# Gates' sums beside the down products, sample loads on ScalarE's queue, earlier prompt loads

## Chip, cores and metric

The kernel runs on one core of one Trainium2 chip. The metric is the time of one execution on the device in microseconds (us). The median of three runs before the change is 2212.91 us.

## The reference

One layer of a hybrid decoder for 1024 prompt tokens and 32 sample tokens (8 sequences of 4), which have 2048 past positions each in pages of 128:

```python
x = x + 0.5 * SwiGLU_1(RMSNorm(x))                 # 1024 -> 2816 -> 1024
q, k, v, fl, bg, cg, u = split(RMSNorm(x) @ w_in)   # 24 tiles of 128 columns, and 8 gate logits
logf = log_sigmoid(fl + b_f)                        # per head
# attention: logit[t, s] = q_t . k_s / 8 + sum of logf over s < j <= t
# sample tokens: keys, values and logf of the past come from the pages of page_table;
# suffix = cumsum(logf_past, reverse) - logf_past
y = bg * conv3(cg * u)
x = x + concat(RMSNorm(attn), RMSNorm(y)) @ w_out
x = x + 0.5 * SwiGLU_2(RMSNorm(x))                  # then the final RMSNorm
```

Outputs are the result for prompt and sample tokens, and the new k, v, logf and conv states. The past gates' sums (`suffix`) depend on the inputs alone, on nothing that the layer computes.

## The kernel before

Every product is made of three: each fp32 operand is split into a high and a low part, and `Step.mm3` (L103 to L105) multiplies high by high, high by low and low by high. A weight is loaded by `Step.load` (L78, three buffers `wraw`), ACT makes its high part `wh` (L86), DVE its low part `wl` (L88). Activations are split the same way (L192 on ACT, L193 on DVE). Tokens stand in four chunks of 264 columns.

The program is one stream; a scheduler puts each engine's instructions in order, except PE's order from the mixing stage on, which is written out by hand. Each engine, and each engine's DMA queue, works through its own list in order. SP issues DMAs only; POOL issues its DMAs and the indirect ones (gathers).

1. **Up** (`K.up`): the first feed-forward products; the result goes in pieces of 132 KB to `h1_d` in DRAM, stored by POOL (L326, L331).
2. **Past gates** (L549 to L582): a pool `gp` on the left side, which takes the space of the up operands, so its tiles wait for them. SP loads the page table (`pt`, `ptl`) and `cin`, DVE makes indices, SP spreads them into `idl`. POOL gathers 32 pages of `lf` (L465), four to a buffer R (two buffers); DVE runs a prefix sum over 512 columns (L577), SP stores it to `bs_d` (L582).
3. **Down** (`K.down`): h comes back from `h1_d` through SP (L384), is split, and multiplied by `w2a` in four sections (`DOWN1`): chunk 0 whole; chunks 1 and 2 with f 0 to 12, then with f 12 to 22; chunk 3. Each product is added to x by DVE (L407). `done1` stores x (L597, POOL) and makes the normed operands XH and XL.
4. **Mix** (L612 on): `forget()`, then the 24 tiles of `w_in` as q, k, v and conv projections (`win`, 3 chunks of 352 columns each, PSUM tiles `pg`, three buffers). Between their steps the sample tokens' attention runs over key and value pages: every second page is loaded by SP with a page number from a register (L802, L803), the others by POOL's gathers (L465), six buffers `kvraw`. This is called the sample stretch here.
5. **Prompt attention**: rounds of logits, softmax, turn and weigh; `load_qk` and vt come by POOL, `conv_norm` of chunks 0 and 1 runs at round 9 (`CONV_AT`) with one buffer `co`, loaded by SP (L1087).
6. The projection by `w_out`, then the second up and down.

Of the kernel before, what the change touches and what calls it, by code (L numbers as in the profile page):

```python
# [8 lines left out]
F32 = mybir.dt.float32  # L9
# [53 lines left out]
class Step:  # L63


    def __init__(self, tc, ios):
        self.tc = tc
        self.nc = tc.nc
        self.io = ios
        self.after = None  # L70
        self.turn = 0
        self.nrs = 2
# [355 lines left out]
def kernel(ctx: ExitStack, tc: tile.TileContext, io: dict):  # L428
# [21 lines left out]

    mrow = cp.tile([P, 4 * NS], F32, name="mrow")
    ident = cst[:, C_ID:C_ID + P]

# [83 lines left out]
    nc.sync.dma_start(bf, io["bf"])  # L537
    by_pair(mrow, lambda r: io["cst"][r:r + 8, C_MASKN:C_MASKN + 4 * NS])
    nc.vector.tensor_copy(idb, ident)
    nc.vector.tensor_copy(diag, cst[:, C_DIAG:C_DIAG + P])  # L540
# [10 lines left out]
    with ExitStack() as es:  # L551
        gp = pool(es, "gp", "left")
        nc.sync.dma_start(pt, io["pt"].rearrange("b s -> (b s)").rearrange("(o n) -> o n", o=1)
                          .broadcast_to([P, NB * PAGES]))
        cin = gp.tile([P, 2], I32, name="cin")
        ptl = gp.tile([P, 2, PAGES], I32, name="ptl")
        for b in range(NB):
            nc.sync.dma_start(ptl[32 * (b % 4):32 * (b % 4) + 32, b // 4, :],
                              io["pt"][b:b + 1, :].broadcast_to([32, PAGES]))
        nc.sync.dma_start(cin, io["cin"])  # L560
        nc.vector.tensor_scalar(idx, pt, P, None, ALU.mult)
        nc.vector.tensor_tensor(idx, idx, cin[:, 0:1].broadcast_to([P, NB * PAGES]), ALU.add)
        ido = gp.tile([P, 2, PAGES], I32, name="ido")
        nc.vector.tensor_scalar(ido, ptl, H, None, ALU.mult)
        nc.vector.tensor_tensor(ido.rearrange("p g s -> p (g s)"), ido.rearrange("p g s -> p (g s)"),
                                cin[:, 1:2].broadcast_to([P, 2 * PAGES]), ALU.add)
        idl = gp.tile([P, 2, PAGES], I32, name="idl")
        by_pair(idl, lambda r: ido[r:r + 8])
        for g in range(2):
            last = None  # L570
            for i in range(4):
                R = gp.tile([P, 4, P], F32, tag="R", bufs=2, name="R")
                for s in range(4):
                    col = PAGES - 1 - (4 * i + s)
                    gather(R[:, s, :], io["lf"], idl[:, g, col:col + 1])
                B = gp.tile([P, 512], F32, tag="B", bufs=2, name="B")
                nc.vector.tensor_tensor_scan(B, ones[:, 0:1].broadcast_to([P, 512]),  # L577
                                             R.rearrange("p s k -> p (s k)"),
                                             last if i else 0.0, ALU.mult, ALU.add)
                last = B[:, 511:512]  # L580
                n = 512 if i < 3 else 511
                nc.sync.dma_start(bs_d[g][:, 512 * i + 1:512 * i + 1 + n], B[:, :n])  # L582

    XH = xpool.tile([P, KD, TOK], F32R, name="XH")
    XL = xpool.tile([P, KD, TOK], F32R, name="XL")
    with ExitStack() as es:
        hp = [pool(es, "h1", "left"), pool(es, "h1b", "left")]
        xp = pool(es, "x2")
        K.tmp = pool(es, "t2")

        def x_in(c):
            x = xp.tile([P, KD, CH], F32, tag="x", bufs=2, name="x")
# [12 lines left out]
        K.nrs = 1  # L605
        K.down(io["w2a"], h1_d, hp, x_in, done1, DOWN1, 16, False)
# [3 lines left out]
    K.wps = [K.wp]  # L610

    es_m, es_s = ExitStack(), ExitStack()  # L612
    with ExitStack() as es:
# [31 lines left out]
        def proj(i, kind, t, chunks=range(NMC)):  # L645

            ws = K.weight(io["w_in"][i], D)
            for c in chunks:
# [14 lines left out]
                else:  # L663
# [3 lines left out]
                    nc.vector.tensor_sub(lo, st, hi)  # L667
                    nc.sync.dma_start(io["ko"][t, :, c * MC:(c + 1) * MC], st)
# [11 lines left out]
        def forget():  # L680
# [42 lines left out]
            for n in range(17, 2, -2):  # L723
# [4 lines left out]
                                           ALU.mult, ALU.add)  # L728
            nc.sync.dma_start(io["fo"][0:SEQ, :].rearrange("(j p) h -> p j h", p=P), lf[:, 0:8, :])
            nc.sync.dma_start(io["fo"][SEQ:TOK, :], lf[:NS, 8, :])  # L730
            yield
# [16 lines left out]
            for r in range(2):  # L748
                nc.sync.dma_start(qx_d[:, r, :], CN)
                nc.sync.dma_start(kx_d[:, 2 + r, :], CN)  # L750
            nc.scalar.copy(CHI.bitcast(F32R), C)
            nc.vector.tensor_sub(CLO.bitcast(F32R), C, CHI)
            nc.sync.dma_start(qx_d[:, 2, :], CHI)
            nc.sync.dma_start(qx_d[:, 3, :], CLO)
            nc.vector.tensor_scalar(C, CHI, -1.0, None, ALU.mult)
            nc.vector.tensor_scalar(CN, CLO, -1.0, None, ALU.mult)
            nc.sync.dma_start(kx_d[:, 0, :], C)
            nc.sync.dma_start(kx_d[:, 1, :], CN)

# [147 lines left out]
        def load_qk(h):  # L907
# [10 lines left out]
            return KA, KB, QA, QB  # L918


        def vnew():
# [5 lines left out]
        def conv(ts):  # L927
            for t in ts:
                q = nc.gpsimd if t == 3 else nc.sync
# [4 lines left out]
                nc.sync.dma_start(E_[:, :, 0:2], io["state"][t])  # L934
                ws = K.weight(io["w_in"][16 + t], D)
# [41 lines left out]
        def values():  # L977
            for t in range(NHP):
                ws = K.weight(io["w_in"][8 + t], D)
                for c in range(NMC):  # L980
# [3 lines left out]
                    nc.scalar.copy(st, ps)  # L984
                    nc.sync.dma_start(v_d[t][:, cs], st[:, :n])
                    nc.sync.dma_start(io["vo"][t, :, c * MC:(c + 1) * MC], st)
                    if n < MC:
# [75 lines left out]
        ap_ = pool(es_a, "ap", "left")  # L1063
        qk = {0: load_qk(0)}
        for n, _ in enumerate(work):
# [3 lines left out]
    for t in range(NHP):  # L1069
        nc.gpsimd.dma_start(at_d[t][:, SEQ:TOK], atS[:, t, :])  # L1070


    es_l, es_r = ExitStack(), ExitStack()
    opc = pool(es_r, "op_c")
    xo = [None] * NCH
    with ExitStack() as es:
# [4 lines left out]
        K.tmp = pool(es, "tb")  # L1081

        def conv_norm(c, co, ps=None):

            cs = slice(c * CH, (c + 1) * CH)
            for t in range(4):
                nc.sync.dma_start(co[:, t, :], co_d[t][:, cs])  # L1087
# [63 lines left out]

        vs, prs, pts = {}, {}, {}
        rounds = [(h, m) for h in range(H) for m in range(4)]

        def front(r):

            if r < len(rounds):
                h, m = rounds[r]
                prs[r] = [logits(h, 2 * m + b) for b in range(2)]
                if m == 0 and h + 1 < H:  # L1160
                    qk[h + 1] = load_qk(h + 1)
                if m == 0 and h % 2 == 0:
                    vt = ap_.tile([P, SEQ], F32, tag="vt", bufs=1, name="vt")
                    nc.gpsimd.dma_start(vt, v_d[h // 2])
                    vs[h // 2] = vt

# [14 lines left out]
        for r in range(len(rounds)):  # L1181
            front(r + 1)
            middle(r)
            back(r - 1)
            if r == CONV_AT:
                for c in range(NCH // 2):
                    conv_norm(c, K.tmp.tile([P, 4, CH], F32, tag="co", bufs=1, name="co"),
                              ptr.tile([P, 512], F32, tag="tr", bufs=3, name="pco")[:, :CH])
# [20 lines left out]
    with ExitStack() as es:  # L1209
# [51 lines left out]
        def norms(c):  # L1261
            conv_norm(c, op_l.tile([P, 4, CH], F32, tag=f"op{8 + c}", bufs=1, name="co"))
            attn_norm(c)
# [134 lines left out]
```

## Time and profile before

| | us |
|---|---|
| median of 3 runs (2210.3 to 2213.24) | 2212.91 |
| profiled execution | 2214.97 |
| its span | 2213.2 |
| up stage ends, down stage's first product | about 480, 538.8 |
| mixing stage and sample stretch | about 807 to 1190 |
| prompt attention from | about 1193 |

The profiled execution stands 2.1 us above the median. TensorE is busy 94% of the span, at a mean granted clock of 0.971 of full speed. All times in the views count from the span's start. A row of the timeline has start, duration, engine, line and operation, and in brackets how long the engine was idle before it and what ended that. PEclk is the share of full speed granted to TensorE: 0.5 is its lower level (1.2 GHz), 1.0 its higher (2.4 GHz).

### The profile page before, as it was taken

Reading aid. Unit: us, or ns where it says so; the run is one execution under the profiler, and the core shown is the slowest. Engines: PE = TensorE matmul, PEld = TensorE weight load, DVE = VectorE, ACT = ScalarE, POOL = GpSimd, SP = SyncE. Lnnn points to the kernel's source line nnn. Section 1 sums busy time; section 2 is a strip of 40 time slices with the busy share of each in tenths; the row PEclk is TensorE's granted clock in tenths of the full one; section 3 lists DMA queues with packets and bytes.
Section 4 is the critical chain, followed back from the end, with each engine's and each line's share of the span. In section 5 each row is a group of like instructions: output and inputs, shape, how many; then the busy total and the mean of one; then the engine's idle time right before and its main releaser. Section 6 shows DMA issues by size and latency. Waiting matters only on the chain.

```text
span 2213.2 us, 44598 instructions
## 1 busy us (share of the span) xinstructions
PE 2070.6 (94%) x17570; PEld 1985.6 (90%) x17570; DVE 1351.2 (61%) x2586; ACT 869.2 (39%) x1736; POOL 318.4 (14%) x467
## 2 busy tenths in 40 slices
PE   7999999962999997999997799999999999999998
PEld 7999999962999986888996577989999999999997
DVE  8877777743655663213223675887777777676354
ACT  6533334321533433222112665454333333364343
POOL 0010110124000021433432231000001110100000
PEclk9999999985999998999998999999999999999999
DMA  6222222215755666998895444432222222387354
GB/s 207 87 86 83 96 86 94 88 55 193 227 170 161 207 197 226 339 352 288 263 272 140 102 118 117 146 128 82 73 83 78 83 88 90 113 300 238 99 171 139
DMA packets 139523, 341.04 MB, mean 154 GB/s; under 512 B 28736, under 2 KB 46368, under 8 KB 137776
## 3 DMA queue, kind: packets, MB, share of 16 engines
q1 hardware_dynamic: 111504, 252.38, 35.8%
q0 software_dynamic: 27808, 85.80, 12.0%
q8 instruction: 138, 2.26, 0.4%
q14 instruction: 73, 0.60, 0.1%
HBM read 279.75 MB, written 58.33 MB: 153 GB/s over the span
## 4 chain that ended last, share of the span: by engine, by line
PE 89%; DMA 3%; DVE 2%; issue 2%; ACT 1%; POOL 1%; SPq 1%; DVEq 0%; POOLq 0%; ACTq 0%
PE ps L104 23%; PE ps L105 23%; PE ps L103 23%; PE pg L103 4%; PE pg L105 4%; PE pg L104 4%; PE O L1145 2%; PE sc L839 1%; PE pv L882 1%; PE ptp L1131 1%; POOL R L465 1%; PE S L1112 1%; PE ps L142 1%; PE S L1113 1%; DMA vt<-v_d 1%
## 5 line engine op out<-in xcount | busy, mean ns | idle before, releaser
L105 PE MATMUL ps<-op,wl 128*128 128x264 f32 x2604 | 742.6, 285 | 0.0
L104 PE MATMUL ps<-op,wh 128*128 128x264 f32 x2604 | 740.8, 285 | 0.5 <-DVE op L193 0.5
L103 PE MATMUL ps<-op,wh 128*128 128x264 f32 x2604 | 739.0, 284 | 0.7 <-ACT op L192 0.4
L86 ACT CAST wh<-wraw 128x512 fp32r<-128x512 f32 x542 | 316.7, 600 | 504.6 <-PE ps L104 304.3
L88 DVE TENSOR_TENSOR wl<-wraw,wh 128x512 fp32r<-128x512 f32 x542 | 351.3, 662 | 231.6 <-ACT wh L86 198.4
L103 PEld LDWEIGHTS ps<-op,wh 128*128 128x128 f32 x2604 | 490.4, 189 | 1.5 <-ACT op L192 0.6
L104 PEld LDWEIGHTS ps<-op,wh 128*128 128x128 f32 x2604 | 489.2, 188 | 1.2 <-DVE op L193 0.9
L105 PEld LDWEIGHTS ps<-op,wl 128*128 128x128 f32 x2604 | 489.3, 188 | 0.2
L103 PE MATMUL ps<-h,wh 128*128 128x264 f32 x1408 | 403.5, 287 | 60.2 <-ACT h L192 58.7
L105 PE MATMUL ps<-h,wl 128*128 128x264 f32 x1408 | 399.7, 284 | 3.3 <-DVE wl L88 3.2
L104 PE MATMUL ps<-h,wh 128*128 128x264 f32 x1408 | 401.7, 285 | 0.2 <-DVE h L193 0.2
L103 PEld LDWEIGHTS ps<-h,wh 128*128 128x128 f32 x1408 | 266.2, 189 | 60.8 <-ACT h L192 58.9
L105 PEld LDWEIGHTS ps<-h,wl 128*128 128x128 f32 x1408 | 266.3, 189 | 4.0 <-DVE wl L88 3.9
L104 PEld LDWEIGHTS ps<-h,wh 128*128 128x128 f32 x1408 | 266.1, 189 | 0.7 <-DVE h L193 0.5
L103 PE MATMUL pg<-XH,wh 128*128 128x352 f32 x576 | 190.7, 331 | 12.6 <-ACT wh L86 12.6
L104 PE MATMUL pg<-XL,wh 128*128 128x352 f32 x576 | 187.7, 326 | 0.0
L105 PE MATMUL pg<-XH,wl 128*128 128x352 f32 x576 | 187.4, 325 | 0.3 <-DVE wl L88 0.3
L86 ACT CAST wh<-s 128x512 fp32r<-128x512 f32 x176 | 107.9, 616 | 120.3 <-PE ps L104 109.9
L103 PEld LDWEIGHTS pg<-XH,wh 128*128 128x128 f32 x576 | 109.4, 190 | 29.8 <-issue 14.9
L88 DVE TENSOR_TENSOR wl<-s,wh 128x512 fp32r<-128x512 f32 x176 | 120.5, 689 | 23.7 <-ACT wh L86 18.6
L326 POOL DMA_DIRECT2D h_d<-t x79 | 42.6, 540 | 601.0 <-DVE t L325 601.0
L105 PEld LDWEIGHTS pg<-XH,wl 128*128 128x128 f32 x576 | 109.1, 189 | 0.8 <-DVE wl L88 0.8
(275 smaller groups left out, 2572.9 us busy)
## 6 DMA issues: line engine op xcount, KB each, us to landing
wraw<-in_w2a SPq DMA_DIRECT2D x48, 512.0 KB
wraw<-in_w2b SPq DMA_DIRECT2D x48, 512.0 KB
h_d<-t POOLq DMA_DIRECT2D x176, 132.0 KB
h<-h_d SPq DMA_DIRECT2D x88, 264.0 KB
kvraw<-in_kc SPq DMA_DIRECT2D x64, 256.0 KB
kvraw<-in_vc SPq DMA_DIRECT2D x64, 256.0 KB
wraw<-in_w1a SPq DMA_DIRECT2D x28, 512.0 KB
wraw<-in_w3a SPq DMA_DIRECT2D x28, 512.0 KB
```

The source lines that it names most:

```text
L86: nc.scalar.copy(wh, x)
L88: nc.vector.tensor_sub(wl, x, wh)
L103: nc.tensor.matmul(ps, w[0], x[0], start=start, stop=False)
L104: nc.tensor.matmul(ps, w[0], x[1], start=False, stop=False)
L105: nc.tensor.matmul(ps, w[1], x[0], start=False, stop=stop)
L142: nc.tensor.matmul(ps, self.ones, sq, start=n == 0, stop=n == len(xs) - 1)
L326: nc.gpsimd.dma_start(h_d[2 * p + 1][:, f, :], t)
L465: nc.gpsimd.indirect_dma_start(out=dst, out_offset=None, in_=src, in_offset=bass.IndirectOffsetOnAxis(ap=ix, axis=0))
L839: nc.tensor.matmul(ps[quarter(hp)], QZ[:, g, hp, 32 * b4:32 * b4 + 32], raw[:, :, hp * P:hp * P + P], start=b4 == 0, stop=b4 == 3)
L882: nc.tensor.matmul(pv[quarter(hp), cs], PT[:, 4 * j + s, quarter(hp)], raw[:, s, hp * P:hp * P + P], start=j == 0 and s == 0, stop=False)
L1112: nc.tensor.matmul(S[:, k0:k1], QA[:, qs], KA[:, k0:k1], start=True, stop=False)
L1145: nc.tensor.matmul(O[HD * b + q:HD * b + q + 32], V[:, j, c0 + q:c0 + q + 32], pt[:, j, :], start=j == 0, stop=j == n)
```

## The change

Three things.

**Past gates.** The indices (`ptl`, `cin`, `ido`, `idl`) are made at the start of the up stage. The gathers move into `past_gates()`, called from `done1` of chunk 0 after the store of x: 16 links, each of two gathers into R (one buffer), a prefix sum over 256 columns in place (L588), a copy of its last column (L591) and a store by POOL (L593). `pt` is loaded by POOL. Line numbers of the changed kernel are a few higher: gather L468, wl L89, x L408, pages L806 and L807, h parts L194.

**Sample stretch.** `K.q` is ACT's queue there: weights, and all stores and loads that SP (and for one conv tile POOL) had issued, go to ACT. SP and POOL issue pages only.

**Prompt.** vt of the first pair is loaded right behind the first head's q and k, the later ones at round 2 of an odd head; the conv inputs of chunks 0 and 1 are loaded by POOL at round 5 into a buffer each.

```diff
     def load(self, src, n):
-            self.last = self.nc.sync.dma_start(raw, src).ins
+            self.last = self.q.dma_start(raw, src).ins
...
     by_pair(mrow, lambda r: io["cst"][r:r + 8, C_MASKN:C_MASKN + 4 * NS])
+    ptl, ido = (K.tmp.tile([P, 2, PAGES], I32, name=n) for n in ("ptl", "ido"))
+    for b in range(NB):
+        nc.sync.dma_start(ptl[32 * (b % 4):32 * (b % 4) + 32, b // 4, :],
+                          io["pt"][b:b + 1, :].broadcast_to([32, PAGES]))
+    nc.sync.dma_start(cin, io["cin"])
...
+    by_pair(idl, lambda r: ido[r:r + 8])
...
     K.up(w1, w3, N0A, ops, h1_d)
...
-        for g in range(2):
-            last = None
-            for i in range(4):
-                R = gp.tile([P, 4, P], F32, tag="R", bufs=2, name="R")
-                for s in range(4):
-                    col = PAGES - 1 - (4 * i + s)
-                    gather(R[:, s, :], io["lf"], idl[:, g, col:col + 1])
-                B = gp.tile([P, 512], F32, tag="B", bufs=2, name="B")
-                nc.vector.tensor_tensor_scan(B, ones[:, 0:1].broadcast_to([P, 512]),
-                                             R.rearrange("p s k -> p (s k)"),
-                                             last if i else 0.0, ALU.mult, ALU.add)
-                last = B[:, 511:512]
-                n = 512 if i < 3 else 511
-                nc.sync.dma_start(bs_d[g][:, 512 * i + 1:512 * i + 1 + n], B[:, :n])
...
+        def past_gates():
+            for g in range(2):
+                for i in range(8):
+                    R = K.tmp.tile([P, 2, P], F32, tag="R", bufs=1, name="R")
+                    for s in range(2):
+                        col = PAGES - 1 - (2 * i + s)
+                        gather(R[:, s, :], io["lf"], idl[:, g, col:col + 1])
+                    r = R.rearrange("p s k -> p (s k)")
+                    nc.vector.tensor_tensor_scan(r, ones[:, 0:1].broadcast_to([P, 256]), r,
+                                                 last if i else 0.0, ALU.mult, ALU.add)
+                    last = K.tmp.tile([P, 1], F32, tag="Rl", bufs=2, name="last")
+                    nc.vector.tensor_copy(last, r[:, 255:256])
+                    n = 256 if i < 7 else 255
+                    nc.gpsimd.dma_start(bs_d[g][:, 256 * i + 1:256 * i + 1 + n], r[:, :n])
...
-            nc.gpsimd.dma_start(x_d[c], x)
+            stored = nc.gpsimd.dma_start(x_d[c], x).ins
...
+            if c == 0:
+                with tc.issue_after(stored):
+                    past_gates()
...
+    K.q = nc.scalar
...
-                    nc.sync.dma_start(dst[:, cs], z[:, :n].bitcast(F32))
+                    nc.scalar.dma_start(dst[:, cs], z[:, :n].bitcast(F32))
...
-        qk = {0: load_qk(0)}
+        qk, vs = {0: load_qk(0)}, {0: load_v(0)}
...
+    K.q = nc.sync
...
-                if m == 0 and h % 2 == 0:
-                    vt = ap_.tile([P, SEQ], F32, tag="vt", bufs=1, name="vt")
-                    nc.gpsimd.dma_start(vt, v_d[h // 2])
-                    vs[h // 2] = vt
+                if m == 2 and h % 2 and h + 1 < H:
+                    vs[h // 2 + 1] = load_v(h // 2 + 1)
...
+            if r == CONV_AT - 4:
+                cos = [conv_load(c, K.tmp, f"co{c}", nc.gpsimd) for c in range(NCH // 2)]
```

In the rows below a tile or tensor before the arrow is written, one behind it read; numbers behind a name tell copies of one tensor apart. DVE in the down stage, in the pairs of chunks 1 and 2, before:

```order
L193 TENSOR_TENSOR h<-h 128x528
L88 TENSOR_TENSOR wl<-wraw,wh 128x256
L88 TENSOR_TENSOR wl<-wraw,wh 128x512
L407 SCALAR_TENSOR_TENSOR x<-ps,x 128x264
L88 TENSOR_TENSOR wl<-wraw,wh 128x512
L124 TENSOR_TENSOR acc<-acc,sq 128x264
L407 SCALAR_TENSOR_TENSOR x<-ps,x 128x264
L124 TENSOR_TENSOR acc<-acc,sq 128x264
L88 TENSOR_TENSOR wl<-wraw,wh 128x256
```

and in the changed kernel; the second scan shown (R<-ones,last,R) is the last of the 16:

```order
L588 SCALAR_TENSOR_TENSOR R<-ones,last,R 128x256
L408 SCALAR_TENSOR_TENSOR x<-ps,x 128x264
L591 COPY last<-R 128x1
L89 TENSOR_TENSOR wl<-wraw,wh 128x512
L125 TENSOR_TENSOR acc<-acc,sq 128x264
L408 SCALAR_TENSOR_TENSOR x<-ps,x 128x264
L125 TENSOR_TENSOR acc<-acc,sq 128x264
L194 TENSOR_TENSOR h<-h 128x528
L588 SCALAR_TENSOR_TENSOR R<-ones,last,R 128x256
L89 TENSOR_TENSOR wl<-wraw,wh 128x256
L591 COPY last<-R 128x1
L89 TENSOR_TENSOR wl<-wraw,wh 128x512
```

The scans stand in the middle of the weights' low parts, which are the same as before.

SP in the sample stretch before, where the first k weight stands (wraw<-in_w_in; kvraw are pages, q_d the stored q projection, out_fo the gates, qx_d and kx_d their prefix sums):

```order
L803 ISA
L803 DMA kvraw<-in_kc 128x512
L729 DMA out_fo<-lf 128x8x8
L730 DMA out_fo<-lf 32x8
L672 DMA q_d_93<-zh 128x320
L672 DMA q_d_94<-zl 128x320
L802 TENSOR_LOAD pt
L802 ISA x2
L803 ISA
L803 DMA kvraw<-in_kc 128x512
L78 DMA wraw<-in_w_in 128x1024
L753 DMA qx_d<-T_10212 8x1024
```

and ACT in the changed kernel, around the loads of the first two k weights:

```order
L87 CAST wh<-wraw 128x512
L665 ACTIVATE QZ<-pg 64x4x4 x4
L676 DMA q_d_94<-zl 128x320
L79 DMA wraw<-in_w_in 128x1024
L658 ACTIVATE zh<-pg 128x352
L79 DMA wraw<-in_w_in 128x1024
L733 DMA out_fo<-lf 128x8x8
L734 DMA out_fo<-lf 32x8
L665 ACTIVATE QZ<-pg 64x4x4 x4
L676 DMA q_d_95<-zh 128x320
L676 DMA q_d_96<-zl 128x320
L744 COPY LF<-pl_10241 8x512
```

The loads and stores now stand among ACT's casts (wh), its copies from PSUM (zh and QZ from pg) and no page.

POOL at the end of the pages, before (KA, QA, KB, QB are the q and k of one head, vt the values of two, at_d the attention result of the sample tokens, co_d the conv outputs):

```order
L917 DMA KA<-k_d_97 64x1024
L974 DMA co_d_112<-st 128x352
L917 DMA KA<-k_d_97 64x1024
L917 DMA QA<-q_d_89 64x1024
L974 DMA co_d_112<-st 128x352
L917 DMA QA<-q_d_90 64x1024
L917 DMA KB<-k_d_98 64x1024
L917 DMA KB<-kx_d 4x1024
L917 DMA QB<-q_d_89 64x1024
L917 DMA QB<-qx_d 4x1024
L1164 DMA vt<-v_d_105 128x1024
L1164 DMA vt<-v_d_106 128x1024
```

and in the changed kernel, from the end of the first head's loads:

```order
L921 DMA KB<-k_d_100 64x1024
L921 DMA KB<-kx_d 4x1024
L921 DMA QB<-q_d_91 64x1024
L921 DMA QB<-qx_d 4x1024
L926 DMA vt<-v_d_107 128x1024
L1079 DMA at_d_115<-atS 128x32
L1079 DMA at_d_116<-atS 128x32
L1079 DMA at_d_117<-atS 128x32
L1079 DMA at_d_118<-atS 128x32
```

The load of vt has moved ahead of the sample tokens' stores and of the second head's loads.

## Rows read from the trace of the kernel before

**Rows 1.** The page: busy time, share of the span and instructions of each engine.
```profile
PE 2070.6 (94%) x17570; PEld 1985.6 (90%) x17570; DVE 1351.2 (61%) x2586; ACT 869.2 (39%) x1736; POOL 318.4 (14%) x467
```

**Rows 2.** Waits of PE: waiting line, releaser, us in total, times, longest.
```profile
PE ps L103 <- ACT h L192: 58.7, 1, 58.7
PE ptv L1099 <- DMA vt<-v_d: 14.5, 1, 14.5
PE pg L103 <- ACT wh L86: 12.6, 2, 9.5
...
PE pco L142 <- ACT sq L141: 10.3, 2, 9.5
```

**Rows 3.** Windows: busy PE, PEld, DVE, ACT, POOL (instructions), granted clock, DMA share, GB/s.
```profile
482.00:540.00 58.00, 1.01 (x3) 0.71 (x4) 11.86 (x12) 1.80 (x4) 30.80 (x32) 0.50 0.33 104
540.00:805.00 265.00, 260.25 (x2111) 259.27 (x2111) 161.44 (x294) 121.79 (x225) 1.85 (x4) 0.99 0.61 200
...
880.00:1190.00 310.00, 309.34 (x2870) 276.66 (x2869) 79.22 (x160) 66.35 (x125) 117.69 (x130) 1.00 0.87 280
```

**Rows 4.** The chain of waits, four stretches: start, us, what ran or landed.
```profile
475.89 0.80 SPq L462
...
531.62 1.30 DVE B L577
...
534.63 3.53 DMA h<-h_d
538.16 0.62 ACT h L192
...
869.02 5.37 DMA wraw<-in_w_in
...
1198.61 13.35 DMA vt<-v_d
...
1261.04 2.07 DMA co<-co_d
```

**Rows 5.** Tile R, the gates' pages: duration ns min/median/max, first and last start.
```profile
L465 POOL DMA_INDIRECT R<-in_lf,idl x32: 940/944/1192, 489.7 to 529.0; - x32
```

**Rows 6.** Windows right behind three of the gaps; columns as in rows 3.
```profile
538.80:543.80 5.00, 4.81 (x20) 4.51 (x21) 4.99 (x8) 4.75 (x8) 0.00 (x0) 0.51 1.06 411
849.00:855.00 6.00, 5.13 (x21) 4.85 (x22) 2.23 (x10) 1.56 (x6) 0.18 (x1) 0.72 0.77 238
1211.90:1217.00 5.10, 5.00 (x24) 4.57 (x25) 1.94 (x3) 2.62 (x6) 0.54 (x1) 0.59 0.55 167
```

**Rows 7.** Timeline, up stage: two stores on POOL, and DVE waiting for them.
```profile
457.00 0.54 POOL L326 DMA_DIRECT2D h_d<-t  x1 [13.21 <-DVE t L325]
459.12 0.54 POOL L326 DMA_DIRECT2D h_d<-t  x1 [1.59 <-DVE t L325]
...
459.10 0.43 DVE L329 TENSOR_TENSOR t<-ps,u 128x264 f32<-128x264 f32 x1 [0.27 <-DMA h_d<-t]
...
461.83 0.43 DVE L329 TENSOR_TENSOR t<-ps,u 128x264 f32<-128x264 f32 x1 [0.84 <-DMA h_d<-t]
```

**Rows 8.** Timeline of POOL: one gather beside a scan, and the last but one.
```profile
497.31 1.19 POOL L465 DMA_INDIRECT R<-in_lf,idl  x1 [0.30 <-issue]
...
527.62 1.08 POOL L465 DMA_INDIRECT R<-in_lf,idl  x1 [0.31 <-issue]
```

**Rows 9.** Timeline of DVE in the down stage, where scans will stand.
```profile
626.48 0.42 DVE L407 SCALAR_TENSOR_TENSOR x<-ps,x 128x264 f32<-128x264 f32 x1
...
703.78 0.42 DVE L407 SCALAR_TENSOR_TENSOR x<-ps,x 128x264 f32<-128x264 f32 x1
...
710.09 1.02 DVE L88 TENSOR_TENSOR wl<-wraw,wh 128x256 fp32r<-128x256 f32 x2
711.02 0.43 DVE L407 SCALAR_TENSOR_TENSOR x<-ps,x 128x264 f32<-128x264 f32 x1
```

**Rows 10.** Timeline of SP in the sample stretch: page issues.
```profile
862.55 5.03 SPq L803 DMA_DIRECT2D kvraw<-in_kc  x4
```

More of the change, by code (lines that the diff above doesn't have):

```diff
@@ L71, in __init__ @@
         self.turn = 0
+        self.q = tc.nc.sync
         self.nrs = 2
@@ L451 @@
     mrow = cp.tile([P, 4 * NS], F32, name="mrow")
+    idl = cp.tile([P, 2, PAGES], I32, name="idl")
+    cin = cp.tile([P, 2], I32, name="cin")
     ident = cst[:, C_ID:C_ID + P]
@@ L538 @@
     by_pair(mrow, lambda r: io["cst"][r:r + 8, C_MASKN:C_MASKN + 4 * NS])
+    ptl, ido = (K.tmp.tile([P, 2, PAGES], I32, name=n) for n in ("ptl", "ido"))
[3 more added lines that the diff above has]
+    nc.sync.dma_start(cin, io["cin"])
+    nc.vector.tensor_scalar(ido, ptl, H, None, ALU.mult)
+    nc.vector.tensor_tensor(ido.rearrange("p g s -> p (g s)"), ido.rearrange("p g s -> p (g s)"),
+                            cin[:, 1:2].broadcast_to([P, 2 * PAGES]), ALU.add)
+    by_pair(idl, lambda r: ido[r:r + 8])
     nc.vector.tensor_copy(idb, ident)
@@ L550 @@
     idx = xpool.tile([P, NB * PAGES], I32, name="idx")
[L551 to L568, printed above, removed]
-        for g in range(2):
-            last = None
-            for i in range(4):
-                R = gp.tile([P, 4, P], F32, tag="R", bufs=2, name="R")
-                for s in range(4):
-                    col = PAGES - 1 - (4 * i + s)
-                    gather(R[:, s, :], io["lf"], idl[:, g, col:col + 1])
-                B = gp.tile([P, 512], F32, tag="B", bufs=2, name="B")
-                nc.vector.tensor_tensor_scan(B, ones[:, 0:1].broadcast_to([P, 512]),
-                                             R.rearrange("p s k -> p (s k)"),
-                                             last if i else 0.0, ALU.mult, ALU.add)
-                last = B[:, 511:512]
-                n = 512 if i < 3 else 511
-                nc.sync.dma_start(bs_d[g][:, 512 * i + 1:512 * i + 1 + n], B[:, :n])
+    nc.gpsimd.dma_start(pt, io["pt"].rearrange("b s -> (b s)").rearrange("(o n) -> o n", o=1)
+                        .broadcast_to([P, NB * PAGES]))
+    nc.vector.tensor_scalar(idx, pt, P, None, ALU.mult)
+    nc.vector.tensor_tensor(idx, idx, cin[:, 0:1].broadcast_to([P, NB * PAGES]), ALU.add)
     XH = xpool.tile([P, KD, TOK], F32R, name="XH")
@@ L748, in forget @@
             for r in range(2):
[L749 to L750 removed]
+                nc.scalar.dma_start(qx_d[:, r, :], CN)
+                nc.scalar.dma_start(kx_d[:, 2 + r, :], CN)
             nc.scalar.copy(CHI.bitcast(F32R), C)
             nc.vector.tensor_sub(CLO.bitcast(F32R), C, CHI)
[L753 to L754 removed]
+            nc.scalar.dma_start(qx_d[:, 2, :], CHI)
+            nc.scalar.dma_start(qx_d[:, 3, :], CLO)
             nc.vector.tensor_scalar(C, CHI, -1.0, None, ALU.mult)
             nc.vector.tensor_scalar(CN, CLO, -1.0, None, ALU.mult)
[L757 to L758 removed]
+            nc.scalar.dma_start(kx_d[:, 0, :], C)
+            nc.scalar.dma_start(kx_d[:, 1, :], CN)
             cn = mix.tile([P, NB, NT], F32, name="cn")
@@ L918, in load_qk, with load_v @@
             return KA, KB, QA, QB
+        def load_v(hp):
+            vt = ap_.tile([P, SEQ], F32, tag="vt", bufs=1, name="vt")
+            nc.gpsimd.dma_start(vt, v_d[hp])
+            return vt
         def vnew():
@@ L1081, with conv_load @@
         K.tmp = pool(es, "tb")
+        def conv_load(c, pool_, tag, queue):
+            co = pool_.tile([P, 4, CH], F32, tag=tag, bufs=1, name="co")
+            for t in range(4):
+                queue.dma_start(co[:, t, :], co_d[t][:, c * CH:(c + 1) * CH])
+            return co
         def conv_norm(c, co, ps=None):
             cs = slice(c * CH, (c + 1) * CH)
-            for t in range(4):
-                nc.sync.dma_start(co[:, t, :], co_d[t][:, cs])
             K.norm([co], G_CO, 512, ps, short=c < 3)
@@ L1184 @@
             back(r - 1)
+            if r == CONV_AT - 4:
+                cos = [conv_load(c, K.tmp, f"co{c}", nc.gpsimd) for c in range(NCH // 2)]
             if r == CONV_AT:
                 for c in range(NCH // 2):
-                    conv_norm(c, K.tmp.tile([P, 4, CH], F32, tag="co", bufs=1, name="co"),
+                    conv_norm(c, cos[c],
                               ptr.tile([P, 512], F32, tag="tr", bufs=3, name="pco")[:, :CH])
@@ L1261, in norms @@
         def norms(c):
-            conv_norm(c, op_l.tile([P, 4, CH], F32, tag=f"op{8 + c}", bufs=1, name="co"))
+            conv_norm(c, conv_load(c, op_l, f"op{8 + c}", nc.sync))
             attn_norm(c)
```

16 lines of the change are left out of this document (8 added, 8 removed).

## The prediction

> **What bounds the kernel now.** I read the page first: TensorE is busy 2070.6 of 2213.2 us [rows 1], and the chain that ended last is PE for nearly nine tenths of it. So time is won only where PE stands still, and the second view is the list of what PE waited for [rows 2]. Four waits make most of it: 58.7 us for the first h tile of the down projection, 14.5 for the prompt's vt, 12.6 for projection weights in two waits, and 9.5 of the 10.3 at pco, for the conv norm. The windows by stretch [rows 3] show that the first wait is a hole of the whole chip (PE 1 of 58 us, DVE 12, DMA share 0.33), while from 880 to 1190 PE is busy 309 of 310 us beside DMA at a share of 0.87.
>
> The chain of waits says what fills the hole [rows 4]: index DMAs on SP's queue from 475.89, then the page gathers until the last scan at 531.62, and only then, at 534.63, the transfer of the first h tile. Nothing in it needs the products: 32 gathers of 0.944 us, from 489.7 to 529.0 [rows 5], and eight scans stand between the two matmul stages on the queue that also issues h.
>
> **The change, part by part.**
>
> *The block between up and down goes.* Its index work (25 small SP DMAs, of up to 0.80 us [rows 4]) moves into the up stage: at most 25 x 0.80 = 20 us of SP's queue, where SP mostly waits for free weight buffers; I cost it at nothing. If that cover were gone, one weight load would come up to 20 us late. The hole of 58.7 ends, ; h of the first token chunk can be loaded as the up operands come free, while PE does the other chunk's last products. The granted clock after the hole was 0.51 over 5 us [rows 6], so half of those 5 us, 2.45, comes back. That is 61.1. What is late next is the first tile's high and low part, 0.62 for the one [rows 4] and about as much for the other; I leave 1.1: gain **60**.
>
> *The gathers' new place: 16 links in the down stage.* Each link is two gathers into the one buffer R, a 256-wide scan in place, and a store on POOL; the next gathers write R, so they wait until the store has landed. I add up one link. Scan: half of 1.30 [rows 4], 0.65. Store start 0.30. Landing: no row has this store; the nearest is the h_d store on POOL. DVE's t waits for it: issued 457.00, go at 459.10, and 459.12 to 461.83 [rows 7]: 2.1 and 2.7, I take 2.35. Gathers to scan: from the last but one at 527.62 [rows 8] to 531.62 [rows 4], 4.0. With 0.2 for hand-overs L = 7.5. From below: with the landing free, 5.15. From above: the upper landing 2.7, and at each scan 1.1 for two DVE instructions ahead in the order, 8.9. I take 7.5, nearest to the stores' own rows.
>
> DVE runs in order, and the scans stand among the weights' low parts. Scan 2 stands behind the scales of chunk 0, before the x at 626.48 [rows 9]. Fourteen links on, scan 16 starts at 626.5 + 14 x 7.5 = 731.5 in the time frame of before. It stands just ahead of the low part made at 710.09 [rows 9], which PE needs about 6.7 later, one pair of products on (x at 703.78 and 711.02 are one pair apart, 7.24). So PE must wait: 731.5 + 0.6 - 716.8 = 15.3, with the copy behind it 16. New waits of PE bring low clock again (behind a 3.1 wait that ended at 849.6 the granted clock was 0.72 over 6 us [rows 6], 1.7 lost); I take 4 for two or three of them. Loss **20**. From 5.15 the chain is covered wholly and costs 0; from 8.9 it costs 36 + 4.
>
> The trace bears one thing against this place: the gather that ran beside a scan took 1.19 us instead of 0.94 [rows 8]. The Trainium skill, "SBUF — State Buffer" (section "SBUF: two separate sides"), says that a DMA issued by GpSimd can be shut out while VectorE holds the port pair that the two share, and gives some 3.1 us for one that takes 0.62 alone. No row here shows more than the 0.25; by the page, one such hit per link would add 2.5 x 14 = 35 us, and the sum would be 43 instead of 77.6.
>
> *The sample stretch.* Weights and stores go from SP to ACT; SP keeps the pages. The second weight wait is SP's order: it stood 5.03 in page issues from 862.55 [rows 10], and the next k weights went out at 869.02, to land 5.37 later [rows 4]. In the new order ACT issues them ahead of those stores, over 20 us sooner. The gain is 12.6, and I count the 1.7 of low clock behind the first wait [rows 6] for each of the two: **16**. Added: 146 issues on ACT, at most 0.54 each as POOL's stores [rows 7], 79 us spread over 380; ACT was busy 66 of 310 in this stretch [rows 3], so I cost them at nothing. If ACT were held, casts of the weights and the emptying of PSUM would stand behind.
>
> That is the added wait: as the program is built, SP's and ACT's DMAs rotate over the same eight completion semaphores, so an ACT issue also waits until the DMA eight before it has landed, which may be a page on SP. Pages landing late hold ACT, with the casts queued behind. The trace shows no such wait on ACT; from below it is 0 (three PSUM buffers, so ACT may be some 10 us late), from above a landing on a loaded ring, 13.35 [rows 4], in place of 5.37. I take **4** in all.
>
> "DMA: Bandwidth & Descriptors" of the Trainium skill (section "Issuing engines are not separate DMA queues") says that issuing from several engines saves only the issue time, as all share 16 DMA engines. By that rule alone the 16 would shrink to under 1 and the sum to 62. I take the row: what was late was the issue, not the transfer.
>
> *Early prompt loads.* vt was issued at 1198.61 behind the second head's loads on POOL, and took 13.35 to land [rows 4]. Now it goes out behind the first head's loads, and the at_d stores, conv stores and second head stand behind it. PE's 14.5 goes, and half of the 5.1 us at clock 0.59 [rows 6], 2.1: **16.6**. Conv inputs for chunks 0 and 1 get buffers of their own, five rounds earlier in the queue; before, the second load was issued at 1261.04, only when the first norm was done, and took 2.07 [rows 4]. The 9.5 go with 1.8 of clock, but the norms' ACT and DVE work still stands before the softmax: I return 2.3 and keep **9**.
>
> Sum: 60 - 20 + 16 - 4 + 16.6 + 9 = 77.6. The profiled execution took 2215.0, 2.1 above the median of 2212.9; 2215.0 - 77.6 = 2137.4, less 2.1 for a median run: forecast **2135 us**.
>
> **Rivals.**
> 1. *Gates covered* (L at or under 6.4, landings short): no wait in the down stage, 20 returned: 2115. For it: 5.15 without the landing. Against: each part of L has a row.
> 2. *Gates longer* (8.9, POOL held by VectorE): 20 more, 2155; for it the gather of 1.19 [rows 8] and a DVE that is busy 161 of 265 us there [rows 3].
> 3. *The stretch gives nothing* (the queue was not the cause): 16 less, 2151; against it the issue at 869.02 [rows 4].
> 4. *ACT partly held*, 0.7 us at each of the 57 chunk products after 880 (of 24 weight tiles five are done by then, the other 19 have three token chunks each): 40 lost in place of 4, 2171. For it: the DMA share of 0.87 in that stretch [rows 3].
> 5. *The other side: ACT held at every chunk.* PE has no idle time there, so each us by which a hold outruns ACT's slack is lost. It decides from (77.6 + 4) / 57 = 1.4 us a chunk; at 1.6, 91 us are lost in place of 4, and the time is 2222, slower than before. For it: the stretch is the one that is full, and landings of 13.35 occur [rows 4]. Against it: SP's queue had all of this in one order, and PE lost nothing from 880 to 1190 [rows 3].
>
> **How the numbers follow.** Forecast 0.48 (2118 to 2150), rival 1 0.13, rival 2 0.13, rival 3 0.06, rival 4 0.11, rival 5 0.09. The range 2105 to 2185 takes in all but rival 5 and the tails of the others. A measurement tells some 0.2% (4.4 us) from no change. Only rival 5 and a small strip below it lie outside faster: faster 0.89, within 0.2% 0.02, slower 0.09.
>
> **What would show it.** Right: PE passes from up to down with under 3 us idle; the first wait of over 3 us of PE is in the down stage, for wl or h behind a scan, with scans 7 to 8 us apart and the last near 670; no PE wait for k weights, vt or co. Wrong: scans at 6 or 9 us (rivals 1, 2); k weights late though issued early (3); PE waiting from 820 to 1130 for ACT's casts, with ACT waiting for page DMAs (4, 5).

## The result, and the profile after

The changed kernel takes 2158.03 us (median of four runs, 2156.09 to 2168.51) beside 2213.07 for the kernel before: a ratio of 0.9762, with a 95% interval of 0.9729 to 0.9795. That is 55 us faster, where 78 were forecast; the time lies in the stated range of 2105 to 2185, but above the 2118 to 2150 that the forecast itself had, and 3 us from the second rival's 2155. The profiled execution has a span of 2154.3 us, 58.9 less than before.

PE executes the same products in the same order in both kernels, so the two traces can be laid side by side: the start of one product in each, and the difference.

| product | before | after | earlier by | won in the stretch | forecast |
|---|---|---|---|---|---|
| late in the first up stage | 474.8 | 470.6 | 4.2 | +4.2 | 0 |
| down stage, section of chunk 0 | 599.0 | 531.2 | 67.9 | +63.7 | +60 |
| down stage, chunk 3 | 780.3 | 760.2 | 20.1 | -47.8 | -20 |
| end of the sample stretch | 1186.0 | 1151.7 | 34.3 | +14.2 | +12 |
| prompt, second half | 1287.7 | 1231.8 | 55.9 | +21.6 | +25.6 |
| last down stage | 2196.9 | 2137.8 | 59.1 | +3.2 | 0 |

Five of the six rows lie within 5 us of their forecast; the gates' links in the down stage cost more than twice their term. The waits of PE in the changed kernel (line, releaser, us in total, times, longest) answer to [rows 2]:

```profile
PE ps L106 <- DVE wl L89: 17.2, 5, 5.4
PE ps L105 <- DVE h L194: 11.9, 1, 11.9
PE ps L164 <- ACT ah L193: 11.3, 2, 11.1
PE ptp L1145 <- ACT PT L1148: 4.7, 2, 3.3
PE ps L104 <- ACT wh L87: 4.5, 2, 2.5
...
PE ps L105 <- DVE last L591: 2.5, 1, 2.5
```

The waits for the first h tile (58.7), for vt (14.5) and for weights of the projections (12.6) are gone, and pco is no longer among the long ones. In their place PE waits for DVE: for low parts of weights and h, and once for the copy that ends a link. The 11.3 us for ACT's ah are no new wait; the kernel before has it too, though the rows ahead of the prediction leave it out: `PE ps L163 <- ACT ah L192: 11.4, 1, 11.4`. The windows of the changed kernel (columns as in [rows 3]) put this into the down stage:

```profile
485.00:745.00 260.00, 223.87 (x1709) 221.40 (x1708) 134.76 (x259) 91.02 (x170) 43.77 (x51) 0.91 0.54 173
...
820.00:1135.00 315.00, 310.82 (x2833) 275.74 (x2831) 83.25 (x172) 71.01 (x142) 116.51 (x126) 1.00 0.88 295
```

PE is busy 224 of 260 us there, at a mean granted clock of 0.91: about 36 us idle, and the rest of the loss is time at the lower clock level behind the waits. (e5, below, is idle for 5.8 us in the same window, at 0.99.) The stretch from 820 is as busy as before, so the other-sign rival did not come.

The timeline of POOL shows two links (start, duration, and in brackets the idle time before and what ended it):

```profile
592.43 0.59 POOL L593 DMA_DIRECT2D bs_d<-R  x1 [2.68 <-DVE last L591]
596.06 0.96 POOL L468 DMA_INDIRECT R<-in_lf,idl  x1 [3.04 <-DMA bs_d<-R]
597.33 0.95 POOL L468 DMA_INDIRECT R<-in_lf,idl  x1 [0.30 <-issue]
600.89 0.59 POOL L593 DMA_DIRECT2D bs_d<-R  x1 [2.62 <-DVE R L588]
605.77 0.96 POOL L468 DMA_INDIRECT R<-in_lf,idl  x1 [4.29 <-DMA bs_d<-R]
```

From the store to the next gather it is 3.63 and 4.88 us; the gathers wait for the store's landing, as the text had it, but over all links this part is 4.08 on average, not 2.55 (the 2.35 landing and 0.2). DVE beside it:

```profile
591.38 0.75 DVE L588 TENSOR_TENSOR_SCAN R<-ones,last,R 128x256 f32<-128x256 f32 x1 [6.06 <-DMA R<-in_lf,idl]
...
593.23 0.68 DVE L89 TENSOR_TENSOR wl<-wraw,wh 128x512 fp32r<-128x512 f32 x1
599.85 0.75 DVE L588 TENSOR_TENSOR_SCAN R<-ones,last,R 128x256 f32<-128x256 f32 x1 [5.94 <-DMA R<-in_lf,idl]
...
600.90 1.28 DVE L89 TENSOR_TENSOR wl<-wraw,wh 128x512 fp32r<-128x512 f32 x2
...
609.55 0.75 DVE L588 TENSOR_TENSOR_SCAN R<-ones,last,R 128x256 f32<-128x256 f32 x1 [6.43 <-DMA R<-in_lf,idl]
```

DVE stands idle for 5.94 us ahead of a scan whose pages have not landed, and the two low parts of weights come out behind it, at 600.90. PE waits for the first of them:

```profile
601.63 0.59 PE L106 MATMUL ps<-h,wl 128*128 128x264 f32 x1 [5.43 <-DVE wl L89]
```

From the second scan at 560.98 to the sixteenth at 693.74 there are 14 links of 9.48 us each.

### The profile page after: what moved, and what is told of

It reads as the page before. It is cut to its first block, busy times and chain, and to the rows that moved or that the text cites. A ratio compares the mean times of both kernels' runs of the same rounds, so it can differ in the third digit from the quotient of the medians.

```text
span 2154.3 us, 44569 instructions
## 1 busy us (share of the span) xinstructions
PE 2067.7 (96%) x17570; PEld 1981.6 (92%) x17570; DVE 1348.8 (63%) x2610; ACT 866.0 (40%) x1736; POOL 332.0 (15%) x487
## 4 chain that ended last, share of the span: by engine, by line
PE 54%; DVE 4%; DMA 2%; ACT 1%; issue 1%; POOL 0%; SPq 0%; ACTq 0%; DVEq 0%; POOLq 0%
PE ps L105 12%; PE ps L104 12%; PE ps L106 11%; PE pg L104 4%; PE pg L105 4%; PE pg L106 4%; PE pv L886 1%; PE sc L843 1%; PE O L1159 1%; DMA wraw<-in_w_out 1%; PE ptp L1145 1%; PE S L1126 1%; PE ps L143 0%; PE S L1127 0%; ACT Pr L1134 0%
## 5 line engine op out<-in xcount | busy, mean ns | idle before, releaser
L89 DVE TENSOR_TENSOR wl<-wraw,wh 128x512 fp32r<-128x512 f32 x542 | 350.7, 663 | 201.8 <-ACT wh L87 176.5
L106 PE MATMUL ps<-h,wl 128*128 128x264 f32 x1408 | 405.3, 288 | 17.2 <-DVE wl L89 17.2
L105 PE MATMUL ps<-h,wh 128*128 128x264 f32 x1408 | 406.5, 289 | 14.3 <-DVE h L194 11.9
L104 PE MATMUL ps<-h,wh 128*128 128x264 f32 x1408 | 408.2, 290 | 4.5 <-ACT wh L87 4.5
L106 PEld LDWEIGHTS ps<-h,wl 128*128 128x128 f32 x1408 | 271.2, 193 | 18.7 <-DVE wl L89 18.6
L105 PEld LDWEIGHTS ps<-h,wh 128*128 128x128 f32 x1408 | 270.8, 192 | 15.2 <-DVE h L194 15.0
L104 PEld LDWEIGHTS ps<-h,wh 128*128 128x128 f32 x1408 | 271.2, 193 | 5.2 <-ACT wh L87 5.0
L89 DVE TENSOR_TENSOR wl<-s,wh 128x512 fp32r<-128x512 f32 x176 | 120.6, 690 | 24.2 <-ACT wh L87 18.9
```

The lines of the kernel that those rows point to most:

```text
L89: nc.vector.tensor_sub(wl, x, wh)
L104: nc.tensor.matmul(ps, w[0], x[0], start=start, stop=False)
L105: nc.tensor.matmul(ps, w[0], x[1], start=False, stop=False)
L106: nc.tensor.matmul(ps, w[1], x[0], start=False, stop=stop)
```

## The experiments

**Theory A:** DVE runs in order; each scan waits for its own link, and the weights behind it wait too. What PE loses is what a link lasts longer than the order leaves it, summed over the links. **Theory B:** the 32 gathers and 16 stores load POOL and the DMA rings, so that weights and h land late whether a scan waits or not. The ratios below are to the kernel before, run on the same chip.

**e1, the scans left out.** The gathered values are stored unsummed; the past gates' sums are not computed.

```diff
-                    nc.vector.tensor_tensor_scan(r, ones[:, 0:1].broadcast_to([P, 256]), r,
-                                                 last if i else 0.0, ALU.mult, ALU.add)
-                    last = K.tmp.tile([P, 1], F32, tag="Rl", bufs=2, name="last")
-                    nc.vector.tensor_copy(last, r[:, 255:256])
```

> The changed kernel with the 16 prefix sums and the copies of their last columns left out (the gathered values are stored unsummed); the 32 gathers and the 16 stores stay, and R still has one buffer. Theory A (DVE runs in order, and a scan that waits for its link holds the weights' low parts behind it): the 48 us that PE lost between 491 and 700 come back almost wholly, about 2113 us (2105 to 2122), and no wait of PE over 3 us in the first down stage before chunk 3. Theory B (the links' DMAs load the rings and POOL, so that weights and h land late whether a scan waits or not): the loss stays, 2145 to 2160.

2121.84 us, 0.9593 (0.9575 to 0.9611). Against B: the DMAs are all there and PE loses nothing until chunk 3. But one wait of 13.4 us is left, at the start of chunk 3, which A had not named. The wait of PE, and DVE's and POOL's timelines of e1:

```profile
PE ps L106 <- DVE wl L89: 13.4, 1, 13.4
```


```profile
692.93 2.92 DVE L190 SCALAR_TENSOR_TENSOR x<-x,prm,rs 128x264 f32<-128x264 f32 x7 [15.46 <-DMA x_d<-x]
```

```profile
687.94 0.59 POOL L589 DMA_DIRECT2D bs_d<-R  x1 [2.04 <-DMA R<-in_lf,idl]
688.52 1.11 POOL L592 DMA_DIRECT2D x_d<-x  x2
```

The store of x of chunk 1 stands behind the whole chain in POOL's queue, and the scaling of x in place waits until it has landed. So the chain's length costs in a second way, once PE is early enough to need that store.

**e2, two buffers for R.**

```diff
-                    R = K.tmp.tile([P, 2, P], F32, tag="R", bufs=1, name="R")
+                    R = K.tmp.tile([P, 2, P], F32, tag="R", bufs=2, name="R")
```

(For the space, `pt` and `idx` are made in the pool `mix` at the start of the mixing stage.)

> R with two buffers (the page table's two tiles are made later, at the start of the mixing stage, for the space). Theory A: a link costs half of a two-link cycle, (4.1 store to gather + 4.0 gather to scan + 1.05 scan to store) / 2 = 4.6 us instead of 9.5, so scan 16 comes at about 626.5 + 14 x 4.6 = 691 in the frame of before; but the scans now stand closer together in DVE's order (the last behind product 20, about 662 in that frame, and some 6 us of slack), so PE still loses about 23 us, mostly early: 2134 us (2122 to 2146). If the loss hung on the DMAs alone (B): 2158 plus or minus 5, as their number is the same. If a buffer were all that mattered and the order nothing: 2113.

2126.76 us, 0.9609 (0.9588 to 0.9629), as A had it. A link takes 5.5 us now (scans 2 and 16 at 553.9 and 631.3), and the scans, which the scheduler put closer together, still wait: PE stands 13.2 us for wl, and loses 18 to 21 us in the down stage instead of 48.

**e3, the links in the up stage.** `past_gates()` is defined and called ahead of `K.up`, and no longer in `done1`.

```diff
+    past_gates()
     K.up(w1, w3, N0A, ops, h1_d)
...
-            if c == 0:
-                with tc.issue_after(stored):
-                    past_gates()
```

> The same 16 links, written ahead of the first up stage, so that they run there and not in the down stage. Theory A: links are about 8 us there (stores landed 2.1 to 2.7 in that stage), the order places the scans some 11 DVE instructions apart, 7 to 8 us; so the order leaves each link about what it needs, and PE loses under 20 us there: 2113 to 2135. Rival: DVE is busy 78% of the up stage and has less slack, each late scan holds the gating that feeds PSUM's release, and the loss is as large or larger, 2150 to 2175. Under B the loss follows the DMAs, and the up stage, with half the DMA load, loses less than 15: 2113 to 2128.

2145.04 us, 0.9689 (0.9669 to 0.9708): between the two ranges, 10 us above what was written down for A and 5 below the rival with less slack. B's 2128 is missed by 17. A link lasts 9.59 us there too (4.13 from store to gather, 4.35 from the first gather to the scan), though the DMA share of that window is 0.24 instead of 0.54. So the order fell short of each link by more than was thought, and PE lost 39 us between 72 and 192 (of the time before). The windows of e3:

```profile
70.00:215.00 145.00, 122.24 (x893) 119.69 (x892) 89.38 (x178) 40.79 (x82) 51.40 (x62) 0.91 0.24 79
215.00:480.00 265.00, 262.56 (x2163) 262.06 (x2162) 196.96 (x410) 93.63 (x215) 29.16 (x54) 1.00 0.29 93
```

It also says that a high DMA share is not what makes a link long. In this stage the same engine stores both kinds of piece: the 16 stores of R to bs_d landed 3.02 us behind their issue in the median, the 18 stores of h beside them 2.10.

**e4, only the weights back on SP.**

```diff
-    K.q = nc.scalar
+    K.q = nc.sync
```

> Only the projection weights of the sample stretch go back to SP's queue, among the pages; all other loads and stores stay on ACT. If the weights' place in SP's queue was the cause of the two waits of 12.6 us: they come back whole or in part, 2160 to 2175. If the waits went because SP was freed from the stores, and not because the weights left it: no change, 2155 to 2161. If ACT's issues held anything that mattered: faster than 2155.

2162.56 us, 0.9765 (0.9743 to 0.9787). By its ratio that is no different from the change (0.9762); by its time it lies 4.5 us above, in the range that stood for waits coming back. The trace decides: PE has no long wait for k weights, and its lead over the kernel before grows from 21.4 to 34.1 us up to 1100 (of the time before), as in the change. SP's queue in e4, where the k weights stand:

```profile
816.92 4.49 SPq L79 DMA_DIRECT2D wraw<-in_w_in  x3
...
840.32 2.57 SPq L807 DMA_DIRECT2D kvraw<-in_kc  x4
845.27 3.28 SPq L79 DMA_DIRECT2D wraw<-in_w_in  x2
```

Pages stand around the weights here too, and yet three were issued by 821.4; in e7, below, with the stores on the same queue, one was issued at 827.31 and the next at 852.67. So the two waits went because SP was freed from the stores and the small loads that went with them. In its profile e4 loses 7 us at 1074: ACT stood 14.06 us on a landing, with PE's next operand behind it. That is not the shared semaphore of the fourth and fifth rivals. The load of a conv state writes E, which has two buffers, and waited until the store out_cso had read the one that it was to fill. The chain of waits of e4:

```profile
1057.99 14.79 DMA out_cso<-E
...
1072.88 0.56 ACTq L943
...
1073.49 0.70 ACT M L894
```

**e5, two buffers and a written order of the scans.** A hook in `K.down` behind each product's addition to x; one link is written at every second product of chunks 1 and 2, its scan queued behind that addition on DVE.

```diff
+                    ins_x = nc.vector.scalar_tensor_tensor(x, o, 0.5, x, ALU.mult, ALU.add).ins
+                    if n and self.link:
+                        self.link(ins_x)
...
+            with tc.issue_after(kept["stored"]):
+                for s in range(2):
+                    gather(R[:, s, :], io["lf"], idl[:, g, col:col + 1])
+            with tc.issue_after(tie):
+                nc.vector.tensor_tensor_scan(r, ones[:, 0:1].broadcast_to([P, 256]), r,
```

> R with two buffers as in e2, and the order of DVE written out: one scan behind every second product of chunks 1 and 2, 8.7 us apart in the first of their sections and 7.2 in the second, where a two-buffer link needs about 4.6 to 5. All 32 gathers, 16 scans, 16 stores are there. Theory A (loss = what a link lasts longer than the order leaves it, summed over the links): no link is late, so nearly all of the 48 us come back and what is left is DVE's own 16 x 1 us, mostly beside PE: 2114 us (2107 to 2122). If the DMAs' load on rings and POOL held weights and h (B): 2125 to 2140, with PE waiting for ACT's wh behind wraw.

2108.92 us, 0.9529 (0.9513 to 0.9545): the fastest of all, 49 us below the change. PE's lead over the kernel before stays at 67.6 us up to chunk 3 and is 70.1 there. Its window and what is left of PE's waits for wl:

```profile
485.00:745.00 260.00, 254.17 (x2067) 251.52 (x2066) 170.34 (x322) 115.73 (x216) 51.16 (x60) 0.99 0.65 212
```

```profile
PE ps L107 <- DVE wl L90: 2.0, 2, 1.8
```

The same 32 gathers, 16 scans and 16 stores in the same stage cost PE nothing that the lead shows. B has fallen.

**e6, the same written order with one buffer.** The diff is that of e5, with `bufs=1` and `pt` in its old place.

> The same written order with one buffer for R, so a link lasts about 9.5 us where the order leaves 8.7 in the first section and 7.2 in the second. Theory A: 7 x 0.8 + 8 x 2.3 = 24 us late at the last scan, less some 6 us of slack: PE loses about 18, 2131 us (2122 to 2142). If only the number of buffers, and not the order, made the difference between the change and e2: as the change, 2158.

2143.46 us, 0.9693 (0.967 to 0.9716). The direction is A's; the size is not: PE lost 32 us, not 18. From the second scan to the fifteenth a link took 10.0 us on average, not 9.5; 6.8 of the loss were taken at the norm behind chunk 1, whose sums also stand behind scans (PE's wait for ah); and the low clock behind the waits was not counted. e6's waits:

```profile
PE ps L106 <- DVE h L195: 10.0, 2, 7.8
PE ps L136 <- ACT ah L134: 9.1, 2, 6.8
PE ps L107 <- DVE wl L90: 8.6, 5, 3.4
```

e5 and e6 differ by a buffer (and by the place of `pt`, which makes room for it), and by 34.5 us. e6 is still 14.6 us faster than the change, with the same single buffer: the order counts as well.

**e7, the whole sample stretch back on SP.** All edits of the second part undone (weights, stores, states; POOL for one conv tile).

> The whole sample-stretch part undone: weights, loads and stores back on SP (and POOL for one conv tile), the rest of the change kept. If the gain of 14 us that the stretch shows comes from the queues: 2158 + 14 = 2172 us (2165 to 2178), with PE waiting for the k weights again. If it came with the earlier parts (other phase of the same queues): 2158 plus or minus 4.

2173.63 us, 0.9816 (0.98 to 0.9833), 15.6 more than the change. The waits for weights are back, 12.1 us in two. SP works through pages, stores and weights in one order, and the weights come late:

```profile
PE pg L104 <- ACT wh L87: 12.1, 2, 9.5
```

```profile
827.31 0.43 SPq L79 DMA_DIRECT2D wraw<-in_w_in  x1
...
846.16 5.10 SPq L807 DMA_DIRECT2D kvraw<-in_kc  x4
852.67 0.52 SPq L79 DMA_DIRECT2D wraw<-in_w_in  x1
```

**e8, vt's load back inside the first round.**

```diff
-        qk, vs = {0: load_qk(0)}, {0: load_v(0)}
+        qk, vs = {0: load_qk(0)}, {}
...
+                if m == 0 and h % 2 == 0:
+                    vs[h // 2] = load_v(h // 2)
```

> Only the load of vt put back to its place inside the first round, behind the second head's loads. If vt's issue was the cause of the 14.5 us wait at the start of the prompt's rounds: 2158 + 14 to 17 = 2173 us (2168 to 2178), PE waiting over 10 us for vt. If the rings being full there was the cause: as the change, 2158 plus or minus 4.

2172.29 us, 0.9821 (0.9805 to 0.9838): 14 more, as expected, but with a wait of only 4.9 us for vt, not over 10 (`PE ptv L1113 <- DMA vt<-v_d: 4.9, 1, 4.9`). The edit puts the loads of the later pairs back too. Of the 13.4 us between the two profiles 3.4 are lost ahead of the prompt, which the edit does not touch, 5.3 at vt's first use with its low clock, and 4.7 in the rounds up to the prompt's second half. So the place of the issue is a cause, but of about 10 us, not of 17; that the first rounds' other loads now come at other times than in the kernel before was not taken apart.

**e10, the conv inputs loaded late.** `conv_load` at `CONV_AT` by SP, one buffer.

```diff
-                    conv_norm(c, cos[c],
+                    conv_norm(c, conv_load(c, K.tmp, "co", nc.sync),
```

> Only the conv inputs of chunks 0 and 1 put back: loaded by SP at the ninth round, one buffer. If that buffer was the cause of the 9.5 us wait at the second norm's sums: 2158 + 7 to 11 = 2167 us (2162 to 2171), PE waiting about 9 us for the square of co. If the norms' own work on ACT and DVE holds the rounds as long: 2155 to 2161.

2178.02 us, 0.9843 (0.9815 to 0.9872), 20 more than the change, out of the expected 7 to 11. The wait named is there, 9.5 us at pco (`PE pco L143 <- ACT sq L142: 10.3, 2, 9.5`); with it came one of 6.3 us at a turn of V behind ACT, and some 4 us had been lost ahead of the prompt. Leaving out what each of the three profiles lost ahead of the stage that was edited (3.0, 3.4 and 4.1), e7, e8 and e10 give back 17, 10 and 15 us, 42 beside the 36 that the two stretches had won; of e10's 15, 10 are lost at pco and 5 at that turn of V, and why the turn came late is not settled.

**e9, e11, e12: the pace of the up stages.** In every changed kernel PE was faster in code that the change does not touch.

> The kernel before, profiled once more. In every profile of the changed kernels PE runs the two up stages, whose code the change leaves as it is, some 0.8% faster than in the profile of before (4.2 us up to 475, 3 us in the second up stage). If that belongs to the one profiled execution: this profile's up stages lie within 1 us of the changed kernel's, and about 7 us of the distance between the two profiles (58.9 us of span against 55 us between the medians) are no effect of the change. If the change makes them faster: this profile agrees with the first one of before within 1 us.

e9 took 2210.75 us in one run; its up stage agrees with the first profile of before. So the pace comes with the change, and is no matter of the one execution. In e11 and e12 the kernel before only gets unused tiles at the place of `idl` and `cin`.

```diff
+    cp.tile([P, 2, PAGES], I32, name="hold1")
+    cp.tile([P, 2], I32, name="hold2")
```

> The kernel before with two unused tiles of 128 and 8 bytes per partition put where the change has its two index tiles, so that everything allocated behind them stands 136 bytes higher in SBUF; not one instruction differs. If the place of the tiles makes TensorE's pace in the two up stages 0.8% faster (seen in every changed kernel): about 7 us faster than before, 2206 us, with the first up stage's last product at 475.5 instead of 480. If the pace comes with another part of the change: as before, 2213 plus or minus 2.

> The same with the 128-byte tile alone. If any shift of the tiles does it: 2206 us. If the 8 bytes beyond a multiple of 128 matter: as before, 2213 plus or minus 2. If place has no effect: both runs at 2213.

e11: 2203.43 us, 0.996 (0.9947 to 0.9974). e12, with the 128 bytes alone: 2209.65 us, 0.9987 (0.9978 to 0.9996). The windows of 200 us in the first up stage, of before, the change, e11 and e12 (busy PE and its matmuls, granted clock, DMA share, GB/s):

```profile
200.00:400.00 200.00, 200.00 (x1639) 1.00 0.28 91
```

```profile
200.00:400.00 200.00, 200.00 (x1652) 1.00 0.28 91
```

```profile
200.00:400.00 200.00, 200.00 (x1653) 1.00 0.29 91
```

```profile
200.00:400.00 200.00, 200.00 (x1643) 1.00 0.28 91
```

PE is never idle and its clock is whole in all four; 13 or 14 products more pass in the same time where the tiles stand 136 bytes higher, and 4 where they stand 128 higher. e9, the kernel before once more, has 1638.

## Why the prediction was right, and where its sum was off

- **The block between up and down** was read rightly: forecast +60, measured +63.7. The first h parts, for which 1.1 us were held back, cost nothing.
- **The links** are the term that was mis-sized: 20 us forecast, 47.8 measured. That PE would wait for parts that stand behind scans held, and so did the last scan's place in DVE's order. The step that failed is the price of a link, "Landing: no row has this store; the nearest is the h_d store on POOL", with 2.35 us for it and 0.2 for all hand-overs. From store to next gather it is 4.08 us on average where 2.55 were taken, from the first gather to the scan 4.39 where 4.0 were, and 1.04 instead of 0.95 from scan to store. That makes 9.5, and (9.48 - 7.5) x 14 = 27.7 is the difference between 20 and 47.8; that it agrees to a tenth is luck. Some 14 us of the loss are time at the lower clock where 4 were held, by an estimate from two windows (223.87 us for the change's 1709 products, 254.17 for e5's 2067). The upper end, 8.9, was too low as well. By the signs that the prediction set down, scans 9 us apart and more are the second rival's.
- **Where the landing's time goes.** In the change a store's data begins to move 1.16 us behind its issue and has moved by 1.67 (medians); with the h_d stores before it is 1.11 and 1.63. But the landing is signalled after 3.3 us (2.5 to 4.8), where the h_d stores have 2.03, and POOL starts the gather 0.76 us behind the signal. So what is longer lies behind the moving. Size and rows do not tell the two stores apart, 128 rows of 1 KB and of 1056 bytes, each into a wider tensor; rows of bs_d begin one element in. Whether that is the reason was not tried.
- **GpSimd's port.** By the Trainium skill, "SBUF — State Buffer" (section "SBUF: two separate sides"), a link could, by an estimate from its 3.1 and 0.62 us, be some 2.5 us longer, from a DMA held beside VectorE; measured were 2.0 more. The number is near, the reason is not shown: the stores begin to move as early as the h_d stores did, and the gathers took 0.964 us in the median instead of 0.944 [rows 5], 1.46 at most in the change. One gather of e3 (3.06 us) and two of e6 (3.38 and 3.79) were that long, beside a busy DVE; what held them was not tried. e1 has 2.8 to 5.7 us from store to next gather with no scan at all.
- **The sample stretch** was right in size (+14.2, forecast 12; the weights' waits gave 17.9 of it, counted at 16), and e7 gives 13.4 of it back in the stretch. Its reason needs a correction: not the weights' place on SP but that of the stores and small loads was the cause (e4 beside e7). The rule of the Trainium skill, "DMA: Bandwidth & Descriptors" (section "Issuing engines are not separate DMA queues"), that more issuing engines save only issue time, would have given under 1 us; here a load stood behind other issues of a queue that was itself waiting, and that is what another queue removes.
- **Holds of ACT by landings** were priced at 4 us, and 3.7 were lost in the change ahead of the first k weight (PE's lead falls from 20.1 to 16.4), 1.7 of them in a wait for ACT's LF; whether a landing held ACT there was not taken apart. The hold that the prediction described came later and cost PE nothing: at 1035 ACT's store of co_d stood on the semaphore that a load of E had used, which took 15.0 us to land (`ACT cg L949 <- DMA E<-in_state: 8.0, 1, 8.0`), and PE's lead stayed at 34.3. e4 shows what a hold of 14 us costs.
- **The prompt**: 21.6 where 25.6 were forecast. At vt's first use 14.8 were won, not 16.6; 2.6 were lost again by 1177, where ACT stood 2.88 us for a weight of `w_out` with the turn's copy PT behind it, a wait that the prediction had not named; and 9.5 came at the norms' sums, for which 9 were forecast. The 3.3 us that PE waited at one softmax behind the norms were made up within 10 us.

```profile
1173.25 0.62 ACT L87 CAST wh<-wraw 128x512 fp32r<-128x512 f32 x1 [2.88 <-DMA wraw<-in_w_out]
1173.77 0.58 ACT L1148 COPY PT<-ptp 128x512 f32<-128x512 f32 x1
```

- **Not in the forecast**: the pace of the two up stages, +4.2 and +3.2, from the place of the tiles in SBUF (e11).

## What to carry to other kernels

A small in-order engine task that waits on a DMA chain costs what the chain is later than the order allows, for every instruction queued behind it: measure the chain's link, then leave it that room in the written order or give it a second buffer, as e5 did with both. When a transfer's latency is not in the trace, a neighbour of the same engine, direction and size can still be 1 us too short (2.03 beside 3.3), so keep the upper end well above it, and price the start of what waits for it. A queue is freed as well by moving what waits in it as by moving what is late.

## What was not expected of the hardware

Moving everything that the kernel before allocates behind `mrow` 136 bytes up in SBUF, with not one instruction changed, made it 9.7 us faster (0.996, 0.9947 to 0.9974). Some 6 us of that are TensorE's pace in the two up stages, 0.9% and 0.6% more products in 200 us, with no idle time and the same clock. A shift of 128 bytes gave about a third of that pace. Why the place matters to the products of these stages and not to those of the down stages, no run here shows.
